# Gated trunk layer on one core: order of the weight sums, two buffers for gates, and the steps around the head of the MLP

## The chip, the cores and the metric

The kernel runs on 1 core of one Trainium2 chip. The time is the device time of one execution in microseconds (us), the median of the runs shown. Lower is better.

## The reference, cut to what matters

One layer of a decoder in float32, for one sequence of 512 tokens, model width 2048 and MLP width 8192:

```python
h = rmsnorm(x, g_mix)
cb, cc, cv, q, k, v, f_logit, gate_c, gate_a = split(h @ w_in)       # widths 1024 x6, 8, 2048, 2048
conv_branch = (cb * causal_dwconv(cc * cv, conv_w)) @ w_conv_out     # 512x1024 @ 1024x2048
attn = forgetting_attention(q, k, v, log_sigmoid(f_logit + b_f))     # 8 heads of 128
attn_branch = attn @ w_attn_out                                      # 512x1024 @ 1024x2048
merged = sigmoid(gate_c + b_gate[:2048]) * conv_branch + sigmoid(gate_a + b_gate[2048:]) * attn_branch
x = x + merged @ w_mix_out                                           # 512x2048 @ 2048x2048
h = rmsnorm(x, g_mlp)
x = x + square(relu(h @ w_ff1)) @ w_ff2                              # 2048 -> 8192 -> 2048
return rmsnorm(x, g_final)
```

The change touches the product with `w_conv_out`, the product with `w_attn_out` and the gates put on both, the product with `w_mix_out`, and the start of the product with `w_ff1`.

## The kernel before

**How a product is computed.** TensorE takes operands in a rounded 32-bit form. Every float32 operand is therefore split in two: a high part `th`, made by ScalarE (a copy that rounds, L103), and a low part `tl`, made by VectorE (operand minus high part, L104). A product is then three matmuls: high by high, high by low, low by high. In `mm_cols` and `mm_rows` the loop `part` runs the two kinds that need only `th` of the weight first (lines 153 and 155, or 172 and 173), and the kind that needs `tl` behind them (157, or 175). A product of a weight tile can so begin when `th` is there, and needs `tl` half way.

**Seven products in place of eight.** Most of the large products are cut into 2x2 blocks and computed with a Strassen-Winograd scheme. The class `Group` does this for one block of 512 columns of a weight: four weight tiles X00, X10, X01, X11 are loaded (`load`, on the queue of SyncE), and seven products are run, named A11, A12, S1, S3, S2, S4, A22. The operands of S1, S3, S2 and of the last are sums of weight tiles that VectorE makes in place (`sub`, L113): the first sum is X01 - X00, written over X00, the operand of S1; X11 - X01, written over X01, is that of S3; the second sum, in the text X01 = X11 - X00 because it is written over X01, is that of S2; and X10 takes X10 minus it for A22. `head` runs A11 and A12; `tail2` runs S1, S3, S2, S4, A22; `tail3`, used for the last column group of `w_mix_out`, runs S1, S2, S4, S3, A22 with fewer tiles live. Results stand in PSUM banks a, b, c, d. ScalarE copies a finished one into an `o` tile (`snap`), VectorE adds another to it (`plus`, L116 is the addition), and `put` takes the finished quarter on. The `o` tiles are a ring of five buffers, which `otile` hands out; every tile named `o`, `hg`, `gt`, or the second `xr` comes from it in the order in which they are asked for.

**The stages around the change.**
- `conv_out(c)` for c = 0 to 3 multiplies the convolution's output with a block of 512 columns of `w_conv_out`. It uses `Columns`, a Group whose weight tiles lie in pairs, and 256-column halves, so the products are short. For c in `GATED` (0 and 3) the gates are loaded ahead (`gates`) and put on here; for c = 1 and 2 the result goes to DRAM ungated (`held_d`).
- `attn_out(c)` for c = 0 to 3 multiplies the attention's output with a block of columns of `w_attn_out`, in two weight chunks of 512 rows (`gemm_t`, `wchunk`), plainly, with three matmuls (L399 to L401). The order is conv 0, attention 0, conv 1, 2, 3, then attention 1, 2, 3 (the text counts them as first to fourth product). As each of the four 128-column results is done, `cons_at(j, ps)` takes it: it loads the attention gate `gt` on SyncE's queue, multiplies (L981) and adds to `merged`. For c not in `GATED` it first loads the convolution gate `hg` on GpSimd's queue (L977) and multiplies `merged` by it (`onto`, L950 or L954). `bring(c)` loads the held convolution output for that.
- `M.quads(c, ...)` makes from `merged` the sums that are the other operand of the next product, and splits them (L904 for one).
- Mix groups g = 0 to 3 multiply with a block of 512 columns of `w_mix_out` (`mm_rows`). `Mix.put` adds the residual rows (`xr`, loaded on GpSimd's queue), takes the squares for the norm, stores the result and puts a transposition on the list `waiting`. `turn` transposes a quarter on TensorE into a PSUM bank (L1082) and copies it into `F`, scaled by the gain (L1091). `Mix.sums` makes the four activation sums of the MLP's scheme from F, and `out` splits each of them (for g < 3 it stores them; for g = 3 it puts them straight into the operand `Q2`).
- `ff1(0)`, in the text the head of the MLP, is the first column group of `w_ff1`. The last quarter of mix group 3 is transposed behind its A11, and `mix.sums` and `out` of S1, S3, S2, S4, A22 follow.

**What sets the order.** The five engines run independently and meet by semaphores. Within an engine, instructions run in the order of its program. A planner works that order out from the dependencies and its own modelled costs, save for instructions pinned with `keep_in_program_order` (`first_sum`, the transposes, `split_in_order`). The dictionary `after` of a Group says which steps the code issues behind which of the seven products (`Steps.add`), so it sets where they stand in the program. A load is started as soon as its queue reaches it and its buffer is free. `pc_` and `pm` are the pools of the convolution and of the mix stages; in `pm` the tags `xr` and `s1` are the buffers of the residual rows and of the first activation sum.

## Time and profile before

| | |
|---|---|
| median of 3 runs | 2454.66 us (2454.66 to 2454.85) |
| profiled execution | 2454.27 us, of which the span 2452.6 us |
| granted TensorE clock, mean | 0.997 |
| TensorE matmul busy | 2408.9 us (98%) |
| VectorE busy | 2043.4 us (83%) |
| ScalarE busy | 1202.0 us (49%) |
| GpSimd busy | 279.7 us (11%) |
| read from and written to HBM | 377.6 and 110.1 MB |

How to read the lines: times are in us from the start of the span. PE is TensorE's matmuls, PEld its weight loads, DVE VectorE, ACT ScalarE, POOL GpSimd, SP SyncE. In a timeline, a row has the start, the time busy, the engine, the line of the kernel, the operation, `out<-in` with their tiles and shapes, and how many are merged in the row (x2); the bracket tells the idle time of the engine before it and what ended it (a tile, its engine and line, or a DMA). L103 and L104 are the lines of `split`, L113 and L116 those of `sub` and `add`, so the tile names tell which step is meant. Ends of matmuls are modelled, and a matmul that runs behind others starts before the end shown for the one ahead of it.

### The profile page before, as it was taken

Reading aid. Unit: us, or ns where it says so; the run is one execution under the profiler, and the core shown is the slowest. Engines: PE = TensorE matmul, PEld = TensorE weight load, DVE = VectorE, ACT = ScalarE, POOL = GpSimd, SP = SyncE. Lnnn points to the kernel's source line nnn. Section 1 sums busy time; section 2 is a strip of 40 time slices with the busy share of each in tenths; the row PEclk is TensorE's granted clock in tenths of the full one; section 3 lists DMA queues with packets and bytes.
Section 4 is the critical chain, followed back from the end, with each engine's and each line's share of the span. In section 5 each row is a group of like instructions: output and inputs, shape, how many; then the busy total and the mean of one; then the engine's idle time right before and its main releaser. Section 6 shows DMA issues by size and latency. Waiting matters only on the chain.

```text
span 2452.6 us, 41546 instructions
## 1 busy us (share of the span) xinstructions
PE 2408.9 (98%) x17800; PEld 2263.6 (92%) x17800; DVE 2043.4 (83%) x1725; ACT 1202.0 (49%) x1233; POOL 279.7 (11%) x450
## 2 busy tenths in 40 slices
PE   8999999999999999999999999999999999999998
PEld 8999899999999989899999999999997888888886
DVE  7987777788887768788888898888978888889898
ACT  6444433345555534355656666566655333333334
POOL 0100000111111112112300000000011001100000
PEclk9999999999999999999999999999999999999999
DMA  7664544454656655747855655656587576655763
GB/s 250 184 193 142 156 131 143 138 167 158 211 177 208 225 175 179 245 125 252 303 198 194 228 179 208 225 192 228 182 307 277 168 249 226 237 189 183 246 224 102
DMA packets 286588, 490.92 MB, mean 200 GB/s; under 512 B 11884, under 2 KB 198372, under 8 KB 286020
## 3 DMA queue, kind: packets, MB, share of 16 engines
q1 hardware_dynamic: 236032, 282.15, 36.2%
q0 software_dynamic: 49504, 205.02, 22.4%
q8 instruction: 139, 2.28, 0.4%
q10 hardware_dynamic: 868, 1.10, 0.1%
q14 instruction: 45, 0.37, 0.1%
HBM read 377.60 MB, written 110.10 MB: 199 GB/s over the span
## 4 chain that ended last, share of the span: by engine, by line
PE 47%; DVE 4%; issue 3%; DMA 2%; ACT 1%; POOL 0%; DVEq 0%; POOLq 0%; ACTq 0%
PE a L175 4%; PE a L173 4%; PE a L172 4%; PE a L153 3%; PE a L157 3%; PE a L155 3%; PE d L175 2%; PE d L173 2%; PE d L172 2%; PE d L155 2%; PE d L153 2%; PE d L157 2%; DVE tl L104 2%; PE c L155 1%; PE c L157 1%
## 5 line engine op out<-in xcount | busy, mean ns | idle before, releaser
L104 DVE TENSOR_TENSOR tl<-x,th 128x2048 fp32r<-128x2048 f32 (+1 forms) x280 | 638.9, 2287 | 173.7 <-ACT th L103 158.7
L103 ACT ACTIVATE th<-x 128x2048 fp32r<-128x2048 f32 (+1 forms) x280 | 536.9, 1918 | 495.4 <-DVE x L113 173.8
L113 DVE TENSOR_TENSOR x<-x,x 128x2048 f32<-128x2048 f32 (+1 forms) x160 | 365.7, 2286 | 19.5 <-DMA x<-in_w_in_dram 15.3
L103 ACT ACTIVATE th<-y 128x2048 fp32r<-128x2048 f32 (+1 forms) x109 | 184.9, 1701 | 278.8 <-PE a L173 138.8
L104 DVE TENSOR_TENSOR tl<-y,th 128x2048 fp32r<-128x2048 f32 (+1 forms) x109 | 218.9, 2013 | 29.9 <-ACT th L103 29.4
L172 PE MATMUL a<-th,us 128*128 128x512 f32 x512 | 199.4, 389 | 1.0 <-ACT th L103 1.0
L153 PE MATMUL c<-S,th 128*128 128x256 f32 x848 | 197.8, 278 | 2.4 <-ACT th L103 2.4
L173 PE MATMUL a<-th,us 128*128 128x512 f32 x512 | 199.2, 389 | 0.0
L155 PE MATMUL c<-S,th 128*128 128x256 f32 x848 | 197.2, 278 | 0.0
L153 PE MATMUL a<-S,th 128*128 128x256 f32 x784 | 182.3, 278 | 1.1 <-ACT th L103 1.1
L155 PE MATMUL a<-S,th 128*128 128x256 f32 x784 | 180.8, 276 | 0.0
L153 PEld LDWEIGHTS c<-S,th 128*128 128x128 f32 x848 | 160.3, 189 | 2.8 <-ACT th L103 2.5
L155 PEld LDWEIGHTS c<-S,th 128*128 128x128 f32 x848 | 160.2, 189 | 0.0
L153 PEld LDWEIGHTS a<-S,th 128*128 128x128 f32 x784 | 147.2, 188 | 1.3 <-ACT th L103 1.3
L155 PEld LDWEIGHTS a<-S,th 128*128 128x128 f32 x784 | 147.3, 188 | 0.0
L175 PE MATMUL a<-tl,us 128*128 128x512 f32 x512 | 136.9, 389 | 0.6 <-DVE tl L104 0.6
L153 PE MATMUL b<-A,th 128*128 128x256 f32 x544 | 126.4, 277 | 0.0
L155 PE MATMUL b<-A,th 128*128 128x256 f32 x544 | 126.4, 277 | 0.0
L153 PE MATMUL d<-S,th 128*128 128x256 f32 x544 | 126.3, 278 | 0.0
L153 PE MATMUL a<-A,th 128*128 128x256 f32 x544 | 126.0, 277 | 0.0
L155 PE MATMUL a<-A,th 128*128 128x256 f32 x544 | 125.8, 277 | 0.0
L155 PE MATMUL d<-S,th 128*128 128x256 f32 x544 | 125.8, 277 | 0.0
(378 smaller groups left out, 6057.6 us busy)
## 6 DMA issues: line engine op xcount, KB each, us to landing
x<-in_w_in_dram SPq DMA_DIRECT2D x86, 1024.0 KB, 5.9
x<-in_w_ff_dram SPq DMA_DIRECT2D x64, 1024.0 KB, 8.1
y<-in_w_ff_dram SPq DMA_DIRECT2D x64, 1024.0 KB, 7.9
us<-s_d POOLq DMA_DIRECT2D x48, 1024.0 KB, 9.7
s_d<-rh POOLq DMA_DIRECT2D x32, 896.0 KB, 5.3
s_d<-r POOLq DMA_DIRECT2D x32, 896.0 KB, 5.7
x<-in_w_mix_out_dram SPq DMA_DIRECT2D x16, 1024.0 KB, 7.2
g_d<-o POOLq DMA_DIRECT2D x32, 256.0 KB, 3.0
```

The costliest lines, as they stand in the source:

```text
L103: a = nc.scalar.activation(out=hi, in_=src, func=AF.Copy, scale=one)
L104: b = nc.vector.tensor_tensor(out=lo, in0=src, in1=hi.bitcast(F32), op=ALU.subtract)
L113: return nc.vector.tensor_tensor(out=out, in0=a, in1=b, op=ALU.subtract)
L153: nc.tensor.matmul(o, hi[:, q, js], Sh, start=first and q == 0 and j == 0, stop=False, skip_group_check=True)
L155: nc.tensor.matmul(o, hi[:, q, js], Sl, start=False, stop=False, skip_group_check=True)
L157: nc.tensor.matmul(o, lo[:, q, js], Sh, start=False, stop=q == nq - 1, skip_group_check=True)
L172: nc.tensor.matmul(o, Sh, hi[:, q, :], start=begin and q == 0, stop=False, skip_group_check=True)
L173: nc.tensor.matmul(o, Sl, hi[:, q, :], start=False, stop=False, skip_group_check=True)
L175: nc.tensor.matmul(o, Sh, lo[:, q, :], start=False, stop=q == nq - 1, skip_group_check=True)
```

## The change

1. In `tail2`, with `apart` set (the convolution's groups only), the second weight sum X11 - X00 is written over X00 and no longer over X01; S2 and the sum for A22 read it there.
2. `cons_at` takes the buffers of the convolution gates `hg` from the pool `pm` (tags `xr` and `s1`, in turn) and not from the ring of `o` tiles. That are eight loads, four in the second and four in the third attention product.
3. `mm_late` runs a product in two passes of `mm_rows`: all rows of the operand but the last two, in both kinds of matmul and both blocks, and then the last two. It takes the place of `mm_rows` in mix group 0.
4. In mix group 3 the transposes of one quarter stand between the two blocks of A22 (`mid`), and `turn` takes other banks there; the transposes of the quarter before are issued behind the same products as in the other groups.
5. `first_of` is split from `Mix.sums`: the first activation sum is made on its own. In the head of the MLP it is split and its successor steps reordered: the other sums now come behind the first weight sum.

```diff
--- before.py
+++ after.py
@@ -156,7 +156,7 @@
                     else:
                         nc.tensor.matmul(o, lo[:, q, js], Sh, start=False, stop=q == nq - 1, skip_group_check=True)
 
-    def mm_rows(ps, Sx, hi, lo, first, extra=None, blocks=range(2)):
+    def mm_rows(ps, Sx, hi, lo, first, extra=None, blocks=range(2), qs=None):
 
         nq, w = hi.shape[1], hi.shape[2]
         for b in blocks:
@@ -164,7 +164,7 @@
             begin = first and (b == 0 or len(ps) == 2)
             ts = slice(b * P, (b + 1) * P)
             for part in range(2):
-                for q in range(nq):
+                for q in qs or range(nq):
                     Sh, Sl = (e[:, ts] for e in Sx(q))
                     if extra == "first" and part == 0 and q == 0 and b == 0:
                         nc.tensor.matmul(o[:, :192], Sh, hi[:, q, :192], start=True, stop=False, skip_group_check=True)
@@ -174,6 +174,12 @@
                     else:
                         nc.tensor.matmul(o, Sh, lo[:, q, :], start=False, stop=q == nq - 1, skip_group_check=True)
 
+    def mm_late(ps, Sx, hi, lo, first):
+
+        nq = hi.shape[1]
+        for qs in (range(nq - 2), range(nq - 2, nq)):
+            mm_rows(ps, Sx, hi, lo, first, qs=qs)
+
     def moving(t):
 
         return lambda q: (t[:, 0, q, :], t[:, 1, q, :])
@@ -189,7 +195,7 @@
             self.extra, self.after, self.shift = extra, {} if after is None else after, shift
             self.view, self.cs, self.w, self.ST, self.mm, self.banks = view, (c1, c2), w, ST, mm, banks
             self.put, self.scale, self.at = put, scale, {}
-            self.pinned = False
+            self.pinned, self.mid, self.apart = False, {}, False
             self.nq = view.shape[0] // (2 * P)
 
         def load(self, i, j):
@@ -207,7 +213,11 @@
         def run(self, ps, n, src, first):
             hi, lo = parts([P, self.nq, self.w], self.shift if self.w == HS else 0)
             split(src, hi, lo)
-            if n in self.extra:
+            if n in self.mid:
+                self.mm(ps, self.ST(n), hi, lo, first, blocks=(0,))
+                self.mid[n]()
+                self.mm(ps, self.ST(n), hi, lo, first, blocks=(1,))
+            elif n in self.extra:
                 self.mm(ps, self.ST(n), hi, lo, first, self.extra[n])
             else:
                 self.mm(ps, self.ST(n), hi, lo, first)
@@ -315,15 +325,16 @@
                 tc.keep_in_program_order(third)
             d = self.acc("d")
             self.run(d, "S3", X[0, 1], True)
-            sub(X[0, 1], X[1, 1], X[0, 0])
-            self.done(0, 0)
+            two, other = ((0, 0), (0, 1)) if self.apart else ((0, 1), (0, 0))
+            sub(X[two], X[1, 1], X[0, 0])
+            self.done(*other)
             d1 = self.snap(d, self.scale)
             self.plus(d1, c, self.scale)
             while later:
                 later.pop(0)()
-            self.run(a, "S2", X[0, 1], False)
-            sub(X[1, 0], X[1, 0], X[0, 1])
-            self.done(0, 1)
+            self.run(a, "S2", X[two], False)
+            sub(X[1, 0], X[1, 0], X[two])
+            self.done(*two)
             s2 = self.snap(a)
             self.plus(d1, a, self.scale)
             self.put(1, 1, d1)
@@ -939,7 +950,7 @@
 
         group = Columns(w_conv_out, c * S, c * S + HS, HS, YS.get, mm_cols, tuple((b,) for b in banks), put,
                         extra={"A11": "first", "S3": "first"})
-        group.after["A12"] = group.first_sum
+        group.after["A12"], group.apart = group.first_sum, True
         whole(group)
 
     whole_of = {}
@@ -973,7 +984,7 @@
 
         def cons_at(j, ps):
             if c not in GATED:
-                hg = otile([P, S], "hg")
+                hg = pm.tile([P, S], F32, tag=("xr", "s1")[j % 2], name="hg")
                 nc.gpsimd.dma_start(out=hg, in_=g_d[0, 4 * c + j])
                 onto(c, j, hg, ALU.mult)
             g = otile([P, S], "gt")
@@ -1075,7 +1086,7 @@
         def turn(self, i, j, v):
             g = self.g
             k = 4 * g + 2 * j
-            pt = bank((5, 6, 7, 6 if self.last else 5)[2 * i + j], "ptr").rearrange("p (two s) -> p two s", two=2)
+            pt = bank((5, 2, 7, 6)[2 * i + j] if self.last else (5, 6, 7, 5)[2 * i + j], "ptr").rearrange("p (two s) -> p two s", two=2)
             for par in range(2):
                 for t in range(2):
                     tc.keep_in_program_order(
@@ -1106,10 +1117,13 @@
                 for e, o in enumerate((hi.bitcast(F32), src)):
                     nc.gpsimd.dma_start(out=h_d[:, SPLIT.index(n), e, 2 * g:2 * g + 2], in_=o)
 
+        def first_of(self):
+            self.s1 = pm.tile([P, 2, HS], F32, tag="s1", name="s1")
+            add(self.s1, self.F[1][:, 0], self.F[1][:, 1])
+
         def sums(self):
             (a11, a12), (a21, a22) = ([f[:, par] for par in range(2)] for f in self.F)
-            s1 = pm.tile([P, 2, HS], F32, tag="s1", name="s1")
-            add(s1, a21, a22)
+            s1 = self.s1
             sub(a21, a11, a21)
             sub(a11, s1, a11)
             sub(a12, a12, a11)
@@ -1148,12 +1162,11 @@
                 after.add(n, quads3[n2])
         if g == 3:
             after.add("S1", mix.fourth, lambda: begin_part("A12", 4))
-        for n in ("A11", "S1") if g < 3 else ("A11", "S1", "S3", "A22"):
+        for n in ("A11", "S1"):
             after.add(n, turn_waiting)
-        if g < 3:
-            after.add("A22", turn_first)
+        after.add("A22", turn_first)
         if before:
-            after.add("A11", before.sums)
+            after.add("A11", before.first_of, before.sums)
             for n, part in (("A12", "S1"), ("S1", "S3"), ("S2", "A22")):
                 after.add(n, lambda before=before, part=part: before.give(part))
         if g < 3:
@@ -1164,10 +1177,12 @@
             after.add("S4", lambda: split_part("A11"))
             after.add("S3", lambda: begin_part("S2", 5))
             after.add("A22", lambda: begin_part("S4", 6), lambda: begin_part("A22", 2), lambda: split_part("A12"))
-        group = Group(w_mix_out, g * S, g * S + HS, HS, M.moving, mm_rows, steady(g), mix.put, after=after,
+        group = Group(w_mix_out, g * S, g * S + HS, HS, M.moving, mm_rows if g else mm_late, steady(g), mix.put, after=after,
                       shift=48)
         if g == 0:
             after.add("A11", group.first_sum)
+        if g == 3:
+            group.mid["A22"] = turn_first
         group.head(True)
         (group.tail2 if g < 3 else group.tail3)()
         before = mix
@@ -1242,8 +1257,8 @@
     common, turned = const.tile([P, 1], F32, name="common"), const.tile([P, NT], F32, name="turned")
 
     g0 = ff1(0, ((5,), (0,), (1,), (7,)))
-    g0.after = Steps(A11=[turn_waiting, mix.sums], A12=[lambda: mix.out("S1", mix.parts["S1"]), g0.first_sum,
-                                                        lambda: factors(common, turned)])
+    g0.after = Steps(A11=[turn_waiting, mix.first_of],
+                     A12=[lambda: mix.out("S1", mix.s1), g0.first_sum, mix.sums, lambda: factors(common, turned)])
     g0.head(True)
     for n in SPLIT[1:]:
         mix.out(n, mix.parts[n])
```

## The prediction

> **What bounds the kernel now.** I read the page first (busy times, then its row of slices), next the groups of PE waits in windows cut by stage, and last the timeline of single engines around each wait.
>
> ```profile
> span 2452.6 us, 41546 instructions
> PE 2408.9 (98%) x17800; PEld 2263.6 (92%) x17800; DVE 2043.4 (83%) x1725; ACT 1202.0 (49%) x1233; POOL 279.7 (11%) x450
> ```
>
> PE is busy for 2408.9 of 2452.6 us, and no edit removes a matmul, so the change can only win idle time of PE, or lose some. Cut by stage (first convolution product, second to fourth attention product, mix group 0, head of the MLP; columns: length, busy of PE, PEld, DVE, ACT, POOL, granted clock, DMA share, GB/s):
>
> ```profile
> 863.90:885.60 21.70, 20.14 (x173) 19.55 (x172) 17.05 (x17) 9.95 (x12) 5.61 (x8) 1.00 0.58 186
> 970.70:1037.90 67.20, 65.88 (x290) 53.87 (x289) 52.50 (x75) 21.31 (x23) 14.63 (x22) 1.00 0.78 257
> 1037.90:1073.80 35.90, 31.77 (x246) 30.32 (x245) 32.76 (x32) 16.95 (x21) 3.96 (x6) 0.95 0.31 93
> 1202.40:1246.10 43.70, 37.31 (x306) 36.29 (x305) 36.59 (x37) 25.33 (x37) 6.67 (x9) 0.96 0.79 297
> ```
>
> PE is idle for 1.6, 1.3, 4.1 and 6.4 us in them; in the last two DVE is about as busy as PE, and the clock is not full. All edits lie in these stages, so some 16 us is the most there is to win.
>
> **Second weight sum of the convolution.** PE at the end of product S3 and start of S2, then DVE and ACT at the same place, then PE in the three later convolution products (x8 is one run of matmuls):
>
> ```profile
> 874.66 1.19 PE L157 MATMUL d<-ys,tl 128*128 128x256 f32 x8 [0.32 <-DVE tl L104]
> 877.09 0.39 PE L153 MATMUL a<-ys,th 128*128 128x256 f32 x1 [1.24 <-ACT th L103]
> 877.31 0.28 PE L155 MATMUL a<-ys,th 128*128 128x256 f32 x1
> 877.43 0.28 PE L153 MATMUL a<-ys,th 128*128 128x256 f32 x1
> 872.78 0.69 DVE L934 TENSOR_TENSOR merged<-o,gates 128x512 f32<-128x512 f32 x1 [1.47 <-DMA gates<-g_d]
> 873.38 1.22 DVE L104 TENSOR_TENSOR tl<-y,th 128x1024 fp32r<-128x1024 f32 x1
> 874.64 2.48 DVE L113 TENSOR_TENSOR y<-y,y 128x1024 f32<-128x1024 f32 x2
> 877.07 2.36 DVE L104 TENSOR_TENSOR tl<-y,th 128x1024 fp32r<-128x1024 f32 x2
> 875.98 2.01 ACT L103 ACTIVATE th<-y 128x1024 fp32r<-128x1024 f32 x2 [4.09 <-DVE y L113]
> ...
> 920.09 0.38 PE L153 MATMUL a<-ys,th 128*128 128x256 f32 x1 [0.59 <-ACT th L103]
> 940.48 0.38 PE L153 MATMUL a<-ys,th 128*128 128x256 f32 x1 [0.58 <-ACT th L103]
> 961.87 0.38 PE L153 MATMUL a<-ys,th 128*128 128x256 f32 x1 [1.34 <-ACT th L103]
> 965.12 0.38 PE L153 MATMUL d<-ys,th 128*128 128x256 f32 x1 [0.24 <-ACT th L103]
> ```
>
> Before, the sum X01 = X11 - X00 overwrites the operand of S3, so DVE makes it (874.64) only when S3's split (873.38) has read it. Written over X00 it needs only S1's split, and the new DVE order has it right behind `o<-b`, in the 1.47 us in which DVE waits for `gates`. Its result stands near 872.5 in place of 875.9, ACT's copy near 873.6 in place of 877.0, and the low part follows S3's split at 875.7, so S2 starts when S3 ends. In the second to fourth product there is no such hole: the sum (1.24 us) pushes S3's split back by up to 1.2 us, close to where PE first uses it. That cover is thin; without it each would cost up to 1.2 us. The five brackets sum to 1.24 + 0.59 + 0.58 + 1.34 + 0.24 = 3.99 us. Ends of matmuls are modelled and overlap the next start, so the brackets understate: S3's eight low matmuls, 0.12 us apart as those at 877.31 and 877.43, would let S2 start at 875.6, which is 1.5 us and not 1.24. I take 4.5 us (bounds 2.0 and 4.9), of which 1.9 is in the last product. The 0.32 us on `gates` stays.
>
> **Gates of the attention products in own buffers.** DVE and PE in the second and third of these products, POOL, and the loads' group (its last row is the time to landing, min/median/max):
>
> ```profile
> 995.52 0.76 DVE L954 TENSOR_TENSOR merged<-merged,hg 128x256 f32<-128x256 f32 x2 [2.67 <-DMA hg<-g_d]
> 1001.51 2.28 DVE L104 TENSOR_TENSOR tl<-raw,th 128x2048 fp32r<-128x2048 f32 x1
> 1017.71 0.69 DVE L950 TENSOR_TENSOR merged<-merged,hg 128x512 f32<-128x512 f32 x1 [3.89 <-DMA hg<-g_d]
> 1025.72 0.39 PE L400 MATMUL pt<-act,th 128*128 128x512 f32 x1
> 1027.36 0.50 PE L401 MATMUL pt<-act,tl 128*128 128x512 f32 x1 [1.25 <-DVE tl L104]
> 978.99 0.57 POOL L977 DMA_DIRECT2D hg<-g_d  x1
> DMA to landing us min/median/max: 2.9/5.8/8.7
> 976.00:998.00 22.00, 22.00 (x99) 18.22 (x98) 14.03 (x24) 4.04 (x6) 8.81 (x15) 1.00 1.02 363
> ```
>
> The last gate is asked for late and holds DVE for 3.89 us; the low part of the fourth product's second weight chunk is then late by 1.25 us. With two buffers off the ring, loads go out as soon as the multiply two gates earlier is done, and the last pair lands before it is wanted: 1.4 us of PE (1027.36 against 1025.72 + 0.23) and about 3.9 us of DVE's lag go. What is new: all eight loads pass two buffers in turn, and the new DVE order puts the multiplies by the third product's first two gates ahead of the split at 1001.51, which before had no such load in front. That split ends at 1003.79, about when PE uses it. With a landing of 5.8 us I place the pairs at 982, 989 and 995 (the whole of the stage counted as it stood), and the split ends 1.5 to 2 us ahead of its use; at the worst landing it does not (below). On POOL's queue the residual load `xr` now follows the sixth gate, at some 1007; its first reader is an addition of DVE in mix group 0, after 1041.5, which hides it. On SP the `gt` loads no longer share the ring and go earlier, which pushes one weight chunk back by about 4 us; it is wanted some 25 us later.
>
> **Last operand tiles at the ends of the products in mix group 0.** DVE takes the last gate product, and later the low part of S2; PE starts S3; the clock behind that:
>
> ```profile
> 1041.53 0.68 DVE L981 TENSOR_TENSOR gt<-pt,gt 128x512 f32<-128x512 f32 x1
> 1067.58 2.28 DVE L104 TENSOR_TENSOR tl<-x,th 128x2048 fp32r<-128x2048 f32 x1
> 1060.73 0.39 PE L172 MATMUL d<-th,M 128*128 128x256 f32 x1 [2.12 <-ACT th L103]
> 1061.30:1064.70 3.40, 3.40 (x18) 3.40 (x17) 3.37 (x2) 0.11 (x1) 0.00 (x0) 0.50 0.00 0
> ```
>
> From 1041.53 to 1069.86 DVE runs almost without a hole, and that chain of 28.33 us, not PE, sets when S2's low part begins. It began 3.6 us after PE left the attention (1037.9). With DVE's lag gone it begins 0.3 us after, so S2 comes 3.3 us sooner against PE. The reorder itself puts low parts behind 12 high matmuls in place of 16 and leaves 36 behind them in place of 32: 4 x 0.12 = 0.5 us lost at the chain's end; what it gives, waits of 0.3 and 0.4 us on M, would be gone anyway. Net 2.8 us (bounds 0 and 5.8, all waits of the stage and the half-clocked stretch). The waits before S3 (about 2 us) and on the low parts stay. The stretch at clock 0.50 costs PE some 1.7 us now, but inside that DVE chain, so I add nothing for it.
>
> **Head of the MLP.** PE's waits, and DVE's chain behind the last:
>
> ```profile
> 1203.95 0.63 PE L1082 MATMUL ptr<-ident,o 128*128 128x128 f32 x4 [1.36 <-DVE o L116]
> 1210.83 0.66 PE L1082 MATMUL ptr<-ident,o 128*128 128x128 f32 x4 [0.57 <-ACT f L1091]
> 1225.70 0.58 PE L153 MATMUL c<-S,th 128*128 128x256 f32 x1 [2.44 <-ACT th L103]
> 1233.67 0.35 PE L146 MATMUL d<-S,th 128*128 128x192 f32 x1 [0.92 <-ACT th L103]
> 1240.61 0.38 PE L153 MATMUL a<-S,th 128*128 128x256 f32 x1 [1.10 <-ACT th L103]
> 1218.34 0.69 DVE L116 TENSOR_TENSOR s<-f 128x512 f32<-128x512 f32 x1 [1.50 <-ACT f L1091]
> 1221.41 2.29 DVE L113 TENSOR_TENSOR x<-x,x 128x2048 f32<-128x2048 f32 x1
> 1226.52 2.28 DVE L104 TENSOR_TENSOR tl<-x,th 128x2048 fp32r<-128x2048 f32 x1
> ```
>
> The transposes between the halves of A22, and a bank of their own, take away 1.36 + 0.57 us, so A22 and A11 run 1.9 us sooner. Little of that arrives. The split of A12's stored part on ACT and DVE can come only about 0.7 us sooner (its ACT chain starts at the unmoved first split), so PE waits there for nearly 1 us, which it did not before. `s<-f` comes at 1216.5 (-1.8). The first sum now stands one DVE step further forward (-0.6): 1219.0, and PE's 1225.70 becomes 1223.3. But the split of one more part (0.6) now precedes S1's low part: 1226.52 becomes 1225.5, the next sum 1.6 us sooner, and PE's 1233.67 and 1240.61 move by as much while its waits before them grow. From 1240.61 on PE runs without waiting for a long time, so 1.6 us is what the end sees (bounds 0 and 6.4).
>
> **Sum.** 4.5 + 1.4 + 2.8 + 1.6 = 10.3 us, off the profiled execution's 2454.27 us: 2444.0. The median of the runs is 0.4 above that execution, so 2444.4, given as 2444.
>
> **Rivals.** (1) *The gates' loads are bound by traffic, not by buffers.* For it: 363 GB/s and a DMA share of 1.02 from 976 to 998, while the loads in question land. Then the split after 1001.51 stays where it is, the 1.9 us won in the last convolution product is waited away there, 1.4 and 3.3 do not come and 0.5 is lost: 2.6 + 1.6 - 0.5 = 3.7 us, so 2451. Against it: the load that ends DVE's 3.89 us before 1017.71 lies outside that stretch. The Trainium skill (DMA: Bandwidth & Descriptors, Issuing engines are not separate DMA queues) says the same of all traffic: transfers started by any engine run on the same 16 DMA engines and interleave; by that rule this rival holds, and the trace's loads up to 8.7 us agree with it in this stretch alone.
> (2) *The clock drops more often.* The half-clocked stretch at 1061.3 follows an idle time of 2.12 us, and the head of the MLP (mean clock 0.96) has the other wait over 2 us (2.44). My forecast leaves waits of about 2 us before S3 twice, and shifted; a drop outside DVE's cover costs 3.4 x 0.5 = 1.7 us each: 2446 to 2447. The Trainium skill (TensorE: Matmul & The Clock Gate, Part 1) gives a free-running window of 3413 ns, which agrees with the 3.4 us; its advice in the section HAM oscillation, that idle gaps over some 3.4 us are what to avoid, does not, as gaps of 2.1 and 2.4 us sufficed here.
> (3) *Slower: the two buffers become a chain.* At the worst landing, 8.7 us, and 1.5 to 2.2 us of DVE work between pairs, the first pair, asked for at 978.99, lands at 987.7, the second at 997.9, the third at 1008.8; then the split ends near 1013.9, 10.1 us after 1003.79. Less the 2.6 us of the earlier products PE is 7.5 us late there; later stages still win 1.4 + 2.8 + 1.6, but an idle time that long brings the half clock (+1.7) and DVE's lag back (+3.3 + 0.5): about 2461. From a landing of about 6.5 us on, the split is late at all; at 8 us the change loses. Against it: that landing needs the traffic of 976 to 998 for all pairs.
> (4) *The sums do not come sooner*, if S3's pushed-back splits cost as much as S2 wins (1.2 us in three products, and thin cover): 4.5 becomes about 1, so 2447.5.
>
> **Chances.** Forecast within 3 us 0.56; (1) 0.15; (2) 0.13; (3) 0.07; (4) 0.09. 0.2% is 4.9 us, about what a measurement tells from no change. Faster: forecast, (2), (4) and a little of (1), 0.81; same: most of (1), 0.12; slower: (3), 0.07. The range takes in (1), (2) and (4) above and, below, the higher bounds of two terms: 2440 to 2451.
>
> **What would show it.** Right: no wait on `th` at the starts of S2 in the convolution; no DVE wait of 3 us on `hg` past 1005; no PE wait at the second chunk of any attention product; in group 0 the chain of 28 us starting with PE's end; no wait at the first two transposes past 1200, a new one near 1 us before A12. Wrong: a PE wait on `tl<-raw` in the third attention product (1, 3), or on `tl<-y` in S3 of a convolution product (4), or a stretch at clock 0.50 in the attention or past the two waits named (2).

## The result, and the profile after

| | before | changed |
|---|---|---|
| median of 9 runs each | 2455.90 us (2454.27 to 2459.69) | 2449.74 us (2446.38 to 2454.48) |
| ratio of the times | 1 | 0.9976 (95% interval 0.9966 to 0.9986) |
| profiled execution | 2454.27 us (span 2452.6) | 2448.67 us (span 2447.0) |

The changed kernel is faster by 5.9 us (0.0024 x 2455.9; 3.4 to 8.3 by the interval). The forecast was faster by 10.7 us (2454.66 to 2444). The direction is right, the size is not: the interval ends short of it. The nine executions of a kernel differ by 5 us (before) and 8 us (changed) among themselves, so where the time went is read from stages, between the same matmuls of both traces.

First the two head lines of the changed kernel's page, then the busy times by stage, of the kernel before and behind it of the changed kernel, with these stages: all convolution products with the first attention product, the second to fourth attention product, mix group 0, and from S3 of mix group 3 to S4 of the MLP's first column group (columns as in the prediction).

```profile
span 2447.0 us, 41536 instructions
PE 2408.6 (98%) x17800; PEld 2265.8 (93%) x17800; DVE 2042.7 (83%) x1725; ACT 1203.9 (49%) x1233; POOL 280.4 (11%) x450
```

```profile
863.98:970.66 106.68, 102.14 (x778) 96.08 (x777) 79.79 (x84) 43.94 (x51) 14.81 (x21) 1.00 0.48 160
970.66:1037.92 67.26, 65.94 (x291) 53.91 (x290) 52.56 (x75) 21.31 (x23) 14.63 (x22) 1.00 0.78 257
1037.92:1085.45 47.53, 43.40 (x346) 41.97 (x344) 40.79 (x38) 22.88 (x29) 4.69 (x7) 0.96 0.43 129
1196.99:1246.15 49.16, 42.77 (x354) 41.75 (x353) 41.09 (x41) 29.03 (x42) 9.54 (x14) 0.97 0.82 304
```

```profile
867.35:969.10 101.75, 100.89 (x778) 95.84 (x777) 78.86 (x84) 44.81 (x51) 14.27 (x20) 1.00 0.50 162
969.10:1036.78 67.68, 65.94 (x290) 53.93 (x289) 54.82 (x79) 21.91 (x24) 15.23 (x23) 1.00 0.79 264
1036.78:1081.72 44.94, 40.88 (x346) 40.04 (x344) 37.57 (x34) 21.67 (x28) 4.74 (x7) 1.00 0.44 135
1192.55:1241.44 48.89, 42.72 (x354) 42.07 (x353) 40.70 (x40) 28.98 (x41) 9.56 (x14) 0.97 0.82 303
```

The lengths differ by -4.93, +0.42, -2.59 and -0.27 us: 7.4 us in all, against 4.5 + 1.4 + 2.8 + 1.6 = 10.3 forecast. (Of the 2.59 us in group 0, 0.55 turn out below to belong to this one execution of the kernel before.) Mix groups 1 to 3 between them are another 0.7 us shorter, and the rest after the last stage 0.9 us. Ahead of the first stage, where nothing was changed, the profiled execution is 3.4 us slower than that of before (867.35 against 863.98): a half-clocked stretch of 3.41 us stands at 21.1 us, and from 471 to 508 us PE ran 3 to 4% slower at a granted clock of 1.00. The second shows in the count of matmuls in 10 us, of the kernel before and then of the changed one:

```profile
480.00:490.00 10.00, 10.00 (x91) 10.00 (x90) 9.19 (x5) 4.33 (x3) 1.42 (x2) 1.00 0.38 147
```

```profile
480.00:490.00 10.00, 10.00 (x88) 10.00 (x87) 9.16 (x6) 3.46 (x2) 1.48 (x3) 1.00 0.61 233
```

The timeline of the changed kernel, at the places of the prediction's rows: PE at the start of S2 in the first convolution product; VectorE and PE in the second and third attention product; VectorE's chain and PE in mix group 0; PE and VectorE at the head of the MLP.

```profile
878.89 0.28 PE L153 MATMUL a<-ys,th 128*128 128x256 f32 x1
...
985.37 1.67 DVE L965 TENSOR_TENSOR merged<-merged,hg 128x256 f32<-128x256 f32 x4 [3.74 <-DMA hg<-g_d]
993.81 0.43 DVE L965 TENSOR_TENSOR merged<-merged,hg 128x256 f32<-128x256 f32 x1 [3.18 <-DMA hg<-g_d]
998.92 0.69 DVE L961 TENSOR_TENSOR merged<-merged,hg 128x512 f32<-128x512 f32 x1 [1.01 <-DMA hg<-g_d]
1002.13 2.28 DVE L104 TENSOR_TENSOR tl<-raw,th 128x2048 fp32r<-128x2048 f32 x1
1004.47 0.50 PE L412 MATMUL pt<-act,tl 128*128 128x512 f32 x1 [1.73 <-DVE tl L104]
...
1037.88 0.68 DVE L992 TENSOR_TENSOR gt<-pt,gt 128x512 f32<-128x512 f32 x1
1057.09 0.39 PE L172 MATMUL d<-th,M 128*128 128x256 f32 x1 [1.66 <-ACT th L103]
1063.93 2.29 DVE L104 TENSOR_TENSOR tl<-x,th 128x2048 fp32r<-128x2048 f32 x1
1066.27 0.97 PE L175 MATMUL a<-tl,M 128*128 128x256 f32 x6 [0.89 <-DVE tl L104]
...
1199.72 0.36 PE L172 MATMUL d<-th,M 128*128 128x256 f32 x1 [1.57 <-DVE o L116]
1213.38 0.69 DVE L116 TENSOR_TENSOR s<-f 128x512 f32<-128x512 f32 x1 [1.62 <-ACT f L1102]
1220.14 0.39 PE L153 MATMUL c<-S,th 128*128 128x256 f32 x1 [2.04 <-ACT th L103]
1228.71 0.35 PE L146 MATMUL d<-S,th 128*128 128x192 f32 x1 [2.12 <-ACT th L103]
```

Read it so. S2 of the convolution has no bracket any more. In the third attention product PE has a wait that was not there, 1.73 us on the low part of the second chunk, whose split at 1002.13 stands behind multiplies that wait for gates; the wait of 1.25 us in the fourth product is gone. In group 0 the chain from the last gate product to the end of S2's low part is as long as before (1037.88 to 1066.22, 28.34 us, against 28.33), but begins 1.1 us after PE left the attention in place of 3.6. At the head of the MLP the transposes wait no longer, but A22 itself does, for the same addition on VectorE.

### The profile page after: what moved, and what is told of

Read it like the earlier page. It is cut to its first block, busy times and chain, and to the rows that moved or that the text cites. A ratio compares the mean times of both kernels' runs of the same rounds, so it can differ in the third digit from the quotient of the medians.

```text
span 2447.0 us, 41536 instructions
## 1 busy us (share of the span) xinstructions
PE 2408.6 (98%) x17800; PEld 2265.8 (93%) x17800; DVE 2042.7 (83%) x1725; ACT 1203.9 (49%) x1233; POOL 280.4 (11%) x450
## 4 chain that ended last, share of the span: by engine, by line
PE 84%; DVE 6%; issue 4%; DMA 3%; ACT 1%; POOL 1%; SPq 0%; DVEq 0%; POOLq 0%; ACTq 0%
PE a L157 6%; PE a L153 6%; PE a L155 6%; PE d L153 5%; PE d L155 5%; PE d L157 5%; PE a L173 5%; PE a L175 5%; PE a L172 5%; PE c L153 4%; PE c L155 4%; PE c L157 4%; PE d L175 3%; PE d L172 3%; PE d L173 3%
```

## The experiments

Stage lengths are differences to the profiled execution of before, in us, between the same matmuls; each shows the number of half-clocked stretches of 3.41 us that lie in the stage (the kernel before has one in group 0 and one in the head). They are taken from unrounded times, so the last digit can differ from the rows above.

| kernel | parts | convolution | attention | group 0 | head | ratio (95% interval) |
|---|---|---|---|---|---|---|
| changed | all | -4.93 (0) | +0.43 (0) | -2.60 (0) | -0.27 (1) | 0.9976 (0.9966 to 0.9986) |
| e5_again | all | -4.74 (0) | +0.54 (0) | -2.62 (0) | -1.36 (1) | 0.9971 (0.9961 to 0.9981) |
| e1_conv | 1 | -3.85 (0) | +0.23 (0) | -0.55 (1) | -0.45 (0) | 0.9981 (0.9972 to 0.9990) |
| e2_gates | 2 | +1.13 (0) | +0.13 (0) | -3.09 (0) | -0.43 (1) | 0.9985 (0.9976 to 0.9994) |
| e3_late | 3 | +0.13 (0) | +0.12 (0) | -0.08 (0) | -0.98 (1) | 0.9995 (0.9986 to 1.0004) |
| e4_mlp | 4, 5 | +0.83 (0) | +0.44 (0) | -0.55 (1) | +0.06 (1) | 0.9998 (0.9989 to 1.0007) |
| e6_ring | 1, 3, 4, 5 | -3.57 (0) | +3.01 (1) | -1.11 (1) | -0.01 (1) | 0.9979 (0.9969 to 0.9988) |
| e7_two_parts | 1, 2 | -4.08 (0) | +0.13 (0) | -3.09 (1) | -1.00 (1) | 0.9963 (0.9950 to 0.9976) |
| e9_two_again | 1, 2 | -5.19 (0) | +0.53 (0) | -3.09 (0) | +0.35 (1) | 0.9968 (0.9956 to 0.9980) |
| e10_turns | 1, 2, 4 | -4.23 (0) | -0.45 (0) | -2.52 (1) | -0.88 (1) | 0.9969 (0.9956 to 0.9981) |
| e11_sums | 1, 2, 5 | -5.08 (0) | +0.43 (0) | -3.07 (1) | -1.13 (0) | 0.9974 (0.9964 to 0.9984) |
| e12_no_late | 1, 2, 4, 5 | -4.73 (0) | -0.08 (0) | -3.11 (1) | -0.79 (1) | 0.9965 (0.9953 to 0.9978) |
| e8_split_first | all, and an order on VectorE | -4.97 (0) | +4.87 (1) | -1.10 (1) | -0.11 (1) | 0.9987 (0.9977 to 0.9996) |

What a stage does where no edit reaches it says how far one execution can be read: +0.1 to +1.1 in the convolution (e2, e3, e4), -1.0 to +0.4 in the head (e1, e2, e3, e7, e9), and -0.55 in group 0 (e1 and e4 alike). The last has a cause that shows. From S2's first low matmul to the transposes at the end of group 0, the same matmuls take this long in the kernel before and in e1:

```profile
1069.91:1085.09 15.18, 15.18 (x128) 15.18 (x129) 10.53 (x8) 6.94 (x10) 0.73 (x1) 1.00 0.82 240
```

```profile
1066.72:1081.35 14.63, 14.63 (x128) 14.63 (x129) 10.05 (x8) 6.92 (x10) 0.73 (x1) 1.00 0.84 250
```

PE ran some 4% slower there, at a granted clock of 1.00, in this one execution of the kernel before. So 0.55 us have to be taken off what group 0 seems to win in each kernel that has no such slower stretch in this place itself (e6, e8 and e10 have one).

**One part at a time.** The diffs are the numbered parts of the change, each put alone into the kernel before.

```diff
 # e1_conv
-            sub(X[0, 1], X[1, 1], X[0, 0])
+            two, other = ((0, 0), (0, 1)) if self.apart else ((0, 1), (0, 0))
+            sub(X[two], X[1, 1], X[0, 0])
 ...
```

> The kernel before with part 1 alone (second weight sum over X00 in the convolution). By either theory the four convolution products are about 4.9 us shorter, as in the changed kernel. Theory A (the low part of the second weight chunk in the third attention product is bound by its loads and by VectorE, not by TensorE): TensorE waits that time away there, on `tl<-raw`, and at the end 0 to 1.5 us are left. Theory B (the parts add up): no new wait, and the end is 4 to 5 us sooner.

```profile
1001.48 0.50 PE L402 MATMUL pt<-act,tl 128*128 128x512 f32 x1 [0.77 <-DVE tl L104]
1024.15 0.50 PE L402 MATMUL pt<-act,tl 128*128 128x512 f32 x1 [0.62 <-DVE tl L104]
```

The convolution is 3.9 us shorter, the attention only 0.2 us longer. PE has a new wait of 0.77 us at the third product's second chunk, which theory B did not expect, but waits 0.62 at the fourth's in place of 1.25, so what the convolution wins is not waited away. Theory A falls, and theory B holds in its sum: 4.7 us by the ratio (2.5 to 6.9).

```diff
 # e2_gates
-                hg = otile([P, S], "hg")
+                hg = pm.tile([P, S], F32, tag=("xr", "s1")[j % 2], name="hg")
```

> The kernel before with part 2 alone (convolution gates in two buffers of their own). The forecast's step: the attention stage from 970.7 is 1.4 us shorter, mix group 0 begins with VectorE less late and is 3.3 us shorter, together 4 to 5 us. The rival (two buffers are a chain): VectorE waits over 3 us on `hg` ahead of the third product's split, TensorE waits on `tl<-raw` there, and the attention stage is not shorter, or up to 1 us longer.

```profile
989.87 0.76 DVE L954 TENSOR_TENSOR merged<-merged,hg 128x256 f32<-128x256 f32 x2 [5.25 <-DMA hg<-g_d]
1008.40 0.50 PE L401 MATMUL pt<-act,tl 128*128 128x512 f32 x1 [1.33 <-DVE tl L104]
1041.82 0.68 DVE L981 TENSOR_TENSOR gt<-pt,gt 128x512 f32<-128x512 f32 x1
```

Of the forecast and of the rival, one half each comes out. The attention stage is not shorter (+0.1): VectorE waits 5.25 us on `hg`, and PE waits 1.33 us on `tl<-raw` in the third product, in place of 1.25 in the fourth, which is the rival. And group 0 is 3.1 us shorter, 2.5 with the 0.55 us taken off. That is the forecast's step, with 2.5 us in place of 3.3: VectorE's last gate product begins 1.1 us after PE left the attention (1041.82 - 1040.76), in place of 3.6.

```diff
 # e3_late
-        group = Group(w_mix_out, g * S, g * S + HS, HS, M.moving, mm_rows, steady(g), mix.put, after=after,
+        group = Group(w_mix_out, g * S, g * S + HS, HS, M.moving, mm_rows if g else mm_late, steady(g), mix.put, after=after,
```

> The kernel before with part 3 alone (last two operand tiles at the ends of the products in mix group 0). The forecast's step: VectorE's chain sets the stage, the waits on M go but come back as waits on low parts, and group 0 is 0 to 0.5 us longer. The rival (M was the bound): group 0 is 0.7 us or more shorter, by the waits of 0.34 and 0.40 us on M.

Group 0 is 0.1 us shorter than in the execution of the kernel before, and 0.5 us longer than in e1 and e4, where it is unchanged (-0.08 against -0.55). The forecast's step comes out: the waits on M are gone, waits on low parts of 0.85 and 1.08 us stand in their place, and VectorE's chain sets the stage.

```diff
 # e4_mlp
-            after.add("A11", before.sums)
+            after.add("A11", before.first_of, before.sums)
+        if g == 3:
+            group.mid["A22"] = turn_first
```

> The kernel before with parts 4 and 5 alone (transposes between the blocks of A22, head of the MLP). The forecast's step: 1.6 us shorter by 1246.9. The rival, as the trace of the changed kernel reads: the low part of S1 and the sum behind it come no sooner against the stage's start than before, and the stretch to 1246.9 is 0.3 us shorter, up to 1 us where the half clock does not fall on S3.

The head is as long as before (+0.06), and so is the time. The forecast's 1.6 us did not come.

**The changed kernel once more, and less one part.**

> The changed kernel once more, unaltered. Theory A (the stages win about 8 us, and what is missing at the end is how often TensorE ran at half clock or some 4% slower outside the change): the stretches at 21 to 24 and 471 to 508 us of the first profile are not there again, or elsewhere, the stages from 864 to 1247 win 7 to 9 us against the kernel before, and the ratio is 0.9965 to 0.9975. Theory B (the change itself costs something outside its stages): both stretches are there again, and the ratio stays at 0.9976 or above.

The first stretch came again at 20.6 us, the second did not, but other half-clocked ones came at 307 and 1840 us. The four stages together with the mix groups between them win 8.1 us in both executions (8.09 and 8.07), or 7.5 with the 0.55 us taken off. The ratio came to 0.9971, inside theory A's range. Both theories' signs are partly met. Such stretches also stand at 21 to 23 us in kernels without most of the parts (e2, e4, e7), so no trace shows a cost of the change outside its stages.

```diff
 # e6_ring
-                hg = pm.tile([P, S], F32, tag=("xr", "s1")[j % 2], name="hg")
+                hg = otile([P, S], "hg")
```

> The changed kernel with part 2 undone (gates `hg` from the ring again). By the forecast's steps: the wait of 1.25 us at the fourth product's second chunk is back, VectorE is late again into mix group 0, and 3 to 5 us are lost against the changed kernel. The rival (the two buffers give nothing, since the third product waits 1.7 us on `tl<-raw` because of them): that wait goes, and no more than 1 us is lost.

Here the third product does not wait, and the fourth does, longer than ever, with VectorE held by a gate first:

```profile
1017.66 0.69 DVE L961 TENSOR_TENSOR merged<-merged,hg 128x512 f32<-128x512 f32 x1 [4.96 <-DMA hg<-g_d]
1024.98 2.29 DVE L104 TENSOR_TENSOR tl<-raw,th 128x2048 fp32r<-128x2048 f32 x1
1027.32 0.49 PE L412 MATMUL pt<-act,tl 128*128 128x512 f32 x1 [2.44 <-DVE tl L104]
```

Attention and group 0 together are 4.1 us longer than in the changed kernel (2.6 and 1.5). Some 1.7 of it is a half-clocked stretch that begins at 1027.72, behind the wait of 2.44 us, and 0.56 is PE running slower at the end of group 0 in this execution. Without that last part it is 3.5 us, inside the forecast's 3 to 5; the ratios (0.9979 and 0.9971 on one chip) show 2 us, and their intervals overlap.

```diff
 # e12_no_late
-        group = Group(w_mix_out, g * S, g * S + HS, HS, M.moving, mm_rows if g else mm_late, steady(g), mix.put, after=after,
+        group = Group(w_mix_out, g * S, g * S + HS, HS, M.moving, mm_rows, steady(g), mix.put, after=after,
```

> The changed kernel with part 3 undone (mix group 0 with the operand tiles in the old order). The forecast's step: the reorder costs 0.5 us at the end of VectorE's chain, so mix group 0 is 0.3 to 0.6 us shorter without it, with waits on M of 0.3 us or none. The rival (part 3 is what makes the group shorter): it is 1 us or more longer.

Group 0 is 0.5 us shorter without part 3: -3.11 against -2.60 and -2.62. The five other kernels that have part 2 and not part 3 show -3.09 three times, -3.07, and -2.52 in e10, which has the slower stretch there. The forecast's step holds to the tenth.

**Parts 1 and 2 alone.** The two edits of e1 and e2 together, in two executions with their own runs.

> The kernel before with parts 1 and 2 alone. If parts 3, 4 and 5 give nothing, as they did alone (3: 0 us in the trace; 4 and 5: 0 to 0.9 us up to 1247), this is as fast as the changed kernel, within 1 us. By the forecast's terms (3 counted as part of 2.8, 4 and 5 as 1.6) it is 1 to 2 us slower. Stages: convolution 4.5 to 5 us shorter, attention 0 to 0.5 us longer, mix group 0 at least 2.4 us shorter.

> Parts 1 and 2 alone once more, on one chip with the three below. If the other parts give nothing, its time is within 1.5 us of the changed kernel's ratio (0.996 to 0.9975). The stretch from 1180 to 1247 is as long as before, to within 0.6 us.

They are as fast as the changed kernel: 0.9963 and 0.9968 against 0.9976 and 0.9971, with intervals that overlap. So parts 3, 4 and 5 together give nothing that these runs can tell. The 0.5 us that part 3 loses in group 0 is too little for them to show at the end.

The two executions, with e12 beside them, answer one more question. The row of mix group 0 in e9, and behind it that in e12:

```profile
1035.28:1079.72 44.44, 40.78 (x345) 39.75 (x344) 38.15 (x34) 22.22 (x28) 4.73 (x7) 1.00 0.45 137
```

```profile
1032.95:1077.37 44.42, 41.85 (x345) 41.20 (x344) 38.23 (x34) 22.34 (x28) 4.72 (x7) 0.96 0.46 137
```

One has a half-clocked stretch and the other has none, and they are equally long. In this place the half clock lies inside VectorE's chain and costs nothing, as the prediction assumed.

**The head of the MLP in two parts.** On top of parts 1 and 2, once with part 4 and once with part 5.

```diff
 # e10_turns: part 4
-            pt = bank((5, 6, 7, 6 if self.last else 5)[2 * i + j], "ptr").rearrange("p (two s) -> p two s", two=2)
+            pt = bank((5, 2, 7, 6)[2 * i + j] if self.last else (5, 6, 7, 5)[2 * i + j], "ptr").rearrange("p (two s) -> p two s", two=2)
...
+        if g == 3:
+            group.mid["A22"] = turn_first
 # e11_sums: part 5
-    g0.after = Steps(A11=[turn_waiting, mix.sums], A12=[lambda: mix.out("S1", mix.parts["S1"]), g0.first_sum,
+    g0.after = Steps(A11=[turn_waiting, mix.first_of],
+                     A12=[lambda: mix.out("S1", mix.s1), g0.first_sum, mix.sums, lambda: factors(common, turned)])
```

> Parts 1, 2 and 4 (transposes between the blocks of A22, banks). The forecast's step: the two waits at the transposes (1.36 and 0.57 us) go, and A11 of the MLP starts 1.9 us sooner against the last weight chunk of mix group 3. The rival, read from the trace of the changed kernel: A22 itself has to wait until VectorE has read bank d (`o<-d,o`), so 1.36 us are waited there in place of the transposes; A11 starts 0.3 to 0.6 us sooner, and nothing of it is left at 1247.

> Parts 1, 2 and 5 (first activation sum on its own, the others behind the first weight sum). The forecast's step: S1 starts 0.6 us sooner against the first `s<-f`. The rival: VectorE's chain from `s<-f` to the start of S3 has the same work in another order, 15.33 us in the kernel before and in the changed one; S1 starts sooner, S3 does not, and 0 us are won at 1247.

Rows of PE and VectorE, in three fences: e9 (neither part), e10, e11.

```profile
1200.64 0.63 PE L1083 MATMUL ptr<-ident,o 128*128 128x128 f32 x4 [1.26 <-DVE o L116]
1207.52 0.66 PE L1083 MATMUL ptr<-ident,o 128*128 128x128 f32 x4 [0.58 <-ACT f L1092]
1230.56 0.35 PE L146 MATMUL d<-S,th 128*128 128x192 f32 x1 [2.24 <-ACT th L103]
```

```profile
1198.96 0.36 PE L172 MATMUL d<-th,M 128*128 128x256 f32 x1 [1.48 <-DVE o L116]
1219.77 0.38 PE L153 MATMUL c<-S,th 128*128 128x256 f32 x1 [2.63 <-ACT th L103]
1227.74 0.36 PE L146 MATMUL d<-S,th 128*128 128x192 f32 x1 [0.61 <-ACT th L103]
```

```profile
1211.92 0.69 DVE L116 TENSOR_TENSOR s<-f 128x512 f32<-128x512 f32 x1 [1.66 <-ACT f L1092]
1218.68 0.38 PE L153 MATMUL c<-S,th 128*128 128x256 f32 x1 [2.03 <-ACT th L103]
1227.24 0.36 PE L146 MATMUL d<-S,th 128*128 128x192 f32 x1 [2.09 <-ACT th L103]
```

With part 4 the wait on the addition (`o<-d,o`) stands before A22 in place of the transposes: A22 may not write bank d before VectorE has read it, and the transposes had only stood in the cover of that. From that addition to A11 it is 7.51 us before and 7.18 in e10: 0.33 us won. With part 5 S1 begins 6.76 us behind `s<-f` in place of 7.36, the 0.6 us that was forecast, and S3 does not begin sooner: 15.32 us behind `s<-f` (1227.24 - 1211.92), against 15.33 before (1233.67 - 1218.34) and 15.33 in the changed kernel. What S1 wins, S3 waits. Both rivals hold, and the new wait before A12 that was forecast is in neither trace. The lengths of the head agree: against the kernel before it is 0.5 us shorter on average in the five kernels with neither part, and 0.6 in the eight with one or both. How long the head is from there depends on the half clock: from S3 to S2 it is 7.3 us in the three executions with such a stretch in S3 (changed, e9, e12), and 6.66 in e10 and e11, which have none there.

**Another order in the third attention product.**

```diff
 # e8_split_first
-            nc.vector.tensor_tensor(out=o, in0=o, in1=g.rearrange("p (h s) -> p h s", h=2), op=op)
+            i = nc.vector.tensor_tensor(out=o, in0=o, in1=g.rearrange("p (h s) -> p h s", h=2), op=op)
+            if op == ALU.mult and c == 2:
+                tc.keep_in_program_order(i)
```

> The changed kernel with the multiplies by `hg` of the third attention product kept behind the split of its second weight chunk in VectorE's order. If these multiplies are what makes that split late (it ran at 1002.13, with `th` ready at 1000.05), the split starts near 1000.1, the wait of 1.73 us on `tl<-raw` goes, and 1 to 2 us are won. If the chunk's landing sets it, or the multiplies come too late for mix group 0 now, nothing is won, or up to 1 us lost.

```profile
997.85 2.29 DVE L104 TENSOR_TENSOR tl<-raw,th 128x2048 fp32r<-128x2048 f32 x1
1000.18 0.50 PE L412 MATMUL pt<-act,tl 128*128 128x512 f32 x1 [0.59 <-DVE tl L104]
1020.38 0.69 DVE L961 TENSOR_TENSOR merged<-merged,hg 128x512 f32<-128x512 f32 x1 [6.04 <-DMA hg<-g_d]
1025.99 0.80 PE L412 MATMUL pt<-act,tl 128*128 128x512 f32 x1 [3.74 <-DVE tl L104]
```

The multiplies were most of what made the split late: without them ahead of it, the wait falls from 1.73 to 0.59 us. But the multiplies that come later free the two buffers later. The last gate, issued at 1011.38, then took 9.0 us to land, in place of 3.2 in the changed kernel, VectorE waited 6.04 us for it, and the fourth product's second chunk is 3.74 us late, with a half-clocked stretch behind it. The attention stage is 4.9 us longer than before, and by the ratios (0.9987 against 0.9971 on one chip) some 4 us are lost, more than either branch of the expectation allowed. The wait can be moved along the chain of eight loads; it did not go away.

## Why the prediction was right or wrong

**Direction and bound: right.** PE is as long busy as before (2408.9 and 2408.6 us). In the convolution its idle time falls from 4.5 to 0.9 us. In group 0 it is 4.1 us in both kernels (47.53 - 43.40 and 44.94 - 40.88): in the kernel before, half-clocked and slower matmuls filled time in which PE would else have waited.

**Second weight sum, 4.5 us: right.** The stage is 4.9 and 4.7 us shorter. From the first matmul to S2 the first product is 1.57 us shorter (877.09 - 863.98 against 878.89 - 867.35); 1.5 was the reading that took the spacing of matmuls in place of the bracket. The three kernels without part 1 (e2, e3, e4) ran the stage 0.1 to 1.1 us longer than this execution of the kernel before, so the gain may be somewhat larger still. Of the thin cover of S3's splits 0.4 us at most was missing, in the third convolution product; the wait of 0.2 us in the second stood there before. Rival (4) did not come.

**Gates in own buffers, 1.4 us: wrong; the attention stage is 0.4 to 0.5 us longer.** The step that failed is "with a landing of 5.8 us I place the pairs at 982, 989 and 995 ... and the split ends 1.5 to 2 us ahead of its use". The median of landings was taken for loads that are issued among the `merged` and weight loads. The first two pairs took 7.4 to 8.3 us (the first gate was issued at 977.38 and landed at 985.34), the others about 3. VectorE waited 3.74 and 3.18 us, and the split ended at 1004.41. Besides, the use against which I measured it was that of the kernel before (1003.79), while the convolution's gain brings PE there about 5 us sooner (-4.93): the term was worked out as if its stage began where it had. Each alone brings a part of the wait, 0.77 us with the convolution's gain (e1) and 1.33 with the buffers (e2), against 1.73 together. The landings are rival (1)'s mechanism, in small: 341 GB/s and a DMA share of 0.96 from 974 to 996.

```profile
974.00:996.00 22.00, 22.00 (x99) 18.21 (x97) 12.89 (x21) 5.51 (x5) 9.04 (x14) 1.00 0.96 341
```

The Trainium skill (DMA: Bandwidth & Descriptors, Issuing engines are not separate DMA queues) says that transfers of any engine's queue share the 16 DMA engines, and by that, free buffers alone bring no gate sooner; these landings agree. Rival (1) was wrong in what it took to follow: the fourth product's wait did go and VectorE's lag fell from 3.6 to 1.1 us, since the later loads are outside that stretch. Rival (3), the chain that loses 7.5 us, did not come in the change, but e8 shows its link: one multiply later, the next load later.

**Mix group 0, 2.8 us: the mechanism right, the size too high; 2.05 us.** The table's 2.6 us less 0.55 are 2.5 won by part 2 and 0.5 lost by part 3. The chain of 28.3 us is the same to 0.01 us, and the 0.5 was forecast. The step that failed is the 3.3 us: "With DVE's lag gone it begins 0.3 us after". It begins 1.1 us after, in the changed kernel as in e2, e9 and e12, since VectorE takes the last gate product only after this row and one more gate product with its additions, without a hole between them:

```profile
1035.87 0.69 DVE L104 TENSOR_TENSOR M<-merged,M 128x512 fp32r<-128x512 f32 x1 [0.41 <-ACT M L103]
```

**Head of the MLP, 1.6 us: wrong; parts 4 and 5 give nothing.** Two steps failed. "The transposes between the halves of A22 ... take away 1.36 + 0.57 us": the first wait belonged to the addition that A22 needs as well, and 0.33 us were left. "1226.52 becomes 1225.5 ... PE's 1233.67 [moves] by as much": the chain on VectorE was counted from `s<-f` at -1.8, which came only 0.1 (changed kernel) and 0.3 us (e10) sooner behind that addition; its length, 15.33 us, did not change.

**The sum.** Of 10.3 us, the four stages gave 6.8 and 7.6 in these two executions with the 0.55 us taken off, and 7.5 in both with the mix groups between them. That the two agree is luck: mix groups 1 to 3 differ by -0.6 to +2.5 us in e1, e2, e3, e7 and e9, which change nothing there. The ratios say 5.9 (3.4 to 8.3) and 7.1 us (4.7 to 9.6), and 7.5 lies in both. That the middle of both is lower isn't explained by a cost of the change that any trace shows; the scatter between executions is as large.

**Rival (2), more half-clocked stretches: did not come in the two profiled executions.** The changed kernel shows two and four of them ahead of the one at the end, the kernel before two, the others one to four. In the changed stages it has one each time, in the head, where the kernel before has one in the head and one in group 0; the further ones stand at 21, 307 and 1840 us, where nothing was changed. For the executions without a trace it isn't known.

## What to carry to other kernels

A wait has to be followed to what the next instruction needs: a transposition that waits for VectorE may stand in the cover of a matmul that needs the same thing, and moving it wins nothing. When edits follow each other along one chain, work out each at the time that the ones before it leave, not at the time of the old trace. Where loads stand in a stretch with the DMA engines full, take the landing time of that stretch and not the median; and of five edits, it pays to measure each one alone, as two of these carried the whole gain. A stage that no edit reaches shows what one execution is worth: here group 0 in e1 and e4 told that 0.55 us of a gain lay in the trace of the kernel before.

## What the runs showed of the hardware

Ahead of the one at the end of each program, all 34 half-clocked stretches in the fourteen traces were 3.41 us long. By the traces' records of the clock, those of one execution begin whole multiples of 3.4133 us apart: 48 in the kernel before (1061.30 and 1225.14), 84, 352 and 533 behind the first in e5 (20.58, 307.30, 1222.07, 1839.88). The Trainium skill (TensorE: Matmul & The Clock Gate, Part 1) gives a free-running window of 3413 ns, which agrees.

Which idle time brings one wasn't told by the length of the wait: 1.81 us before S3 of group 0 was followed by one in e6 and e8, while 2.25 us at the same place was followed by one in e4, e7, e10 and e12 and not in e2 and e9. It is told, to about 0.1 us, by how much idle time of PE falls into one window of that grid. In e12, 2.09 of the 2.25 us lie in one window; in e9 the wait is cut into 0.40 and 1.85. From 14 us to the last stretch of each trace (ends of matmuls as modelled), all 25 windows with 1.94 us or more of idle time were followed by a stretch in the next window, none with less than 1.81, and 9 of the 17 between.

Beside these, PE ran 3 to 4% slower for up to 36 us at a granted clock of 1.00 (88 against 91 matmuls in 10 us), which costs up to 1.4 us; such a stretch stood at 110 to 146 us in every execution, and others came and went. What brings them was not tried. Ahead of the first stage, where nothing was changed, one of each kind (about 1.7 and 1.4 us) make up most of the 3.4 us between the two profiled executions.
